# Layer 0's opening products: loads of x in pairs, one modulation run per k tile, and a told order for splits and loads

## The chip, the cores and the metric

The kernel runs on one core of a Trainium2 chip. The metric is device time in microseconds, the median of the runs; a profiled execution of the same program gives the trace. TensorE does the products, VectorE and ScalarE the element-wise work, SyncE issues nearly all loads, and each engine runs its own instructions in order and waits on semaphores for the others.

## What is computed

Two layers of a trunk over 256 latent tokens (x) and 256 context tokens, each 2048 wide. The part that matters here is the front of layer 0: a modulation vector for x and one for the context, the norm, the modulated stream h, and the first columns of h @ w_in.

```python
shift, scale, gate = jnp.split(jax.nn.silu(c) @ w_mod + b_mod, 3, axis=-1)
hx = _rmsnorm(x, norm_w) * (1 + scale[:, None]) + shift[:, None]
a_h, a_b, a_c, a_z, q, k, v, r_z = _split_in(hx @ w_in)
...
mod_c = jax.nn.silu(c_ctx) @ w_mod[:, :n_mod * d] + b_mod[:n_mod * d]
hc = _rmsnorm(ctx, norm_w) * (1 + mod_c[d:2 * d]) + mod_c[:d]
ca_h, ca_b, ca_c, ca_z, cq, ck, cv, cr_z = _split_in(hc @ w_in)
...
y_conv = _conv_branch(a_h, a_b, a_c, a_z, conv_w, conv_norm_w)
x = x + gate[:, None] * (jnp.concatenate([y_conv, y_ret], axis=-1) @ w_out)
```

Conv, retention, w_out and the whole of layer 1 follow, and a last norm.

## The kernel before

**Tiles.** x and the context stand transposed: 16 k tiles (KT) of 128 features by 512 tokens (NT), the first 256 columns x, the others the context. A weight is used as two parts, a high one in fp32r (`whi`, ScalarE's copy of a piece of 1024 columns, 512 at a time) and the rest (`wlo`, VectorE's subtraction); h and y are pairs of the same kind. A product of a 128x128 block of weights with a k tile is three matmuls of 512 columns (`mm3`, L346 to L348): high with high, high with low, low with high.

**The opening (`first_group`, L208).** Seven output tiles of w_in (`p`, in seven PSUM banks) grow side by side over the 16 k tiles, 7 x 16 x 3 = 336 matmuls, while the modulation that h needs is made k tile by k tile. A chunk of the modulation (`MOD_CHUNKS`) has one k tile at both ends and two k tiles between. `mod_step` (L485) multiplies silu(c), silu(c_ctx) with pieces of w_mod as they come, four instructions to a step, each with 32 columns of the array of its own (`tile_position=(0, 32 * j)`) and 256 or 512 columns of weights, in plain fp32; a step reads one piece of 512 KB (`wm`), or two. After four steps ScalarE copies the sums out (`msb`), TensorE transposes them (`modt`, `mod_finish`, L505), and VectorE adds the four parts and the bias (`mv`) and makes the scale (`am`). `h_prep` (L541) then makes xn = x * rstd, scales and shifts it in place per half of the tokens (L548), copies it to h's high part on ScalarE and subtracts for the low part on VectorE (`split`, L368). The statistics (`first_stat`, L458) are 16 squares, summed on VectorE in two sums, and two matmuls with ones.

**Order.** The program names steps; a tile scheduler that puts instructions into an order of its own per engine is free in the whole kernel, so products of p stand between the instructions of one modulation step.

**Loads.** `pump` (L287) issues loads in the order of use (`seq`) into six buffers of 512 KB (`RAW`), each free once its reader is done; splits run up to three pieces ahead (`AHEAD`), with four buffers of high and low halves (`WH`). x comes first, in 16 loads of 256 KB (L387). `load_rest` (L416) fetches constants and a 2 MB broadcast of c and c_ctx (`cb`) at the end of the opening; `silu_rows` (L438) applies silu to it during the first tile behind the opening, since the rows of the later modulation (`mod_row`, VectorE) read it.

**Slots.** x, then yf, x1 and y use 16 slots of 256 KB, one k tile each; h's pairs have 16 of 512 KB.

Of the kernel before, what the change touches and what calls it, by code (L numbers as in the profile page):

```python
# [17 lines left out]
P = 128  # L18
# [65 lines left out]
MOD_CHUNKS = [[0], [1]] + [[2 * i, 2 * i + 1] for i in range(1, 7)] + [[14], [15]]  # L84
# [7 lines left out]
def pack_mod_chunks(w):  # L92
    pieces = []
    for ks in MOD_CHUNKS:
        cols = np.concatenate([mod_tile(w, SCALE + k) for k in ks] + [mod_tile(w, SHIFT + k) for k in ks], axis=1)
        n = cols.shape[1]
        per = 1024 // n
        pieces.append(cols.reshape(KT // per, per, P, n).transpose(0, 2, 1, 3).reshape(KT // per, P, 1024))
    return np.ascontiguousarray(np.concatenate(pieces))
# [24 lines left out]
def layout(x, c, ctx, c_ctx, norm_w, w_mod, b_mod, w_in, conv_w, conv_norm_w, ret_norm_w,  # L124
# [10 lines left out]
    wm = pack_mod_chunks(w_mod[0])  # L135
# [26 lines left out]
    cb = np.concatenate([c[0], c_ctx]).reshape(1, 2 * D)  # L162
# [3 lines left out]
class Trunk:  # L166
    RAW, WH, AHEAD, TMP = 6, 4, 3, 9

    def __init__(self, ctx, tc, io):
# [3 lines left out]
        self.pa = pool("slots", 16)  # L173
# [7 lines left out]
        self.dram = pool("dram", 1, space=bass.MemoryType.DRAM)  # L181

    def slot(self, name, dt=F32):
        return self.pa.tile([P, NT], dt, tag="slot", name=name)
# [12 lines left out]
    def build_program(self):  # L197
# [10 lines left out]
        def first_group():  # L208
            subs = []
            for c, ks in enumerate(MOD_CHUNKS):  # L210
                m = [("M", c, i) for i in range(4)]
                prog.extend(m[:2])
                prog.extend(subs[:-2])
                prog.append(m[2])
                prog.extend(subs[-2:-1])
                prog.extend([m[3], ("MF", c)])
                prog.extend(subs[-1:])
                subs = [("P", 0, k, i) for k in ks for i in range(2)]
            prog.extend(subs)

        for l in range(DEPTH):
            for op in layer_ops(l):
                if op[0] == "P1":
                    if l == 0:
                        first_group()
                    else:
                        prog.extend(("P", 1, k, h) for k in range(KT) for h in range(2))
# [26 lines left out]
        for op in prog:  # L254
            ps = []
            if op[0] == "M":
                n = 2 if len(MOD_CHUNKS[op[1]]) == 2 else 1
                ps = [("wm", (nm + i,)) for i in range(n)]
                nm += n
            elif op[0] == "D":  # L260
                ps = [("wd", (2 * op[1] + op[2],))]
            elif op[0] == "P":
                _, l, k, sub = op
                last = (7 * k + (3 if sub == 0 else 6)) // 8
# [11 lines left out]
        assert nin == [128, 128] and nout == [32, 32] and nm == 64  # L276
# [4 lines left out]
        self.free = [False] * len(seq)  # L281
# [5 lines left out]
    def pump(self):  # L287
        nc = self.nc
        while True:
# [8 lines left out]
            while self.nsplit < 2 * self.nload:  # L298
# [12 lines left out]
                elif s > self.at + self.AHEAD:  # L311
                    break
# [728 lines left out]
```

## Time and profile before

| | |
|---|---|
| median of the runs | 1570.89 us (1570.33 to 1571.09) |
| the profiled execution | 1568.8 us, its span 1567.0 us |
| mean granted TensorE clock | 0.997 |
| TensorE busy | 1535.5 us, 98% of the span |
| VectorE, ScalarE busy | 1153.3 us (74%), 702.0 us (45%) |
| loads and stores | 287.27 MB, mean 183 GB/s |
| loads of x: 16 of 256 KB; of w_mod for the opening: 64 of 512 KB | 5.4 and 6.2 us each to landing |

Times are in us from the first instruction of the span. A busy TensorE is one with a matmul in its pipe: matmuls overlap, and the time that one costs is the distance from its start to the next one's, not its own duration. A plain fp32 instruction leaves two records, so counts of the modulation products are twice the instructions.

### The profile page before, as it was taken

Reading aid. Unit: us, or ns where it says so; the run is one execution under the profiler, and the core shown is the slowest. Engines: PE = TensorE matmul, PEld = TensorE weight load, DVE = VectorE, ACT = ScalarE, POOL = GpSimd, SP = SyncE. Lnnn points to the kernel's source line nnn. Section 1 sums busy time; section 2 is a strip of 40 time slices with the busy share of each in tenths; the row PEclk is TensorE's granted clock in tenths of the full one; section 3 lists DMA queues with packets and bytes.
Section 4 is the critical chain, followed back from the end, with each engine's and each line's share of the span. In section 5 each row is a group of like instructions: output and inputs, shape, how many; then the busy total and the mean of one; then the engine's idle time right before and its main releaser. Section 6 shows DMA issues by size and latency. Waiting matters only on the chain.

```text
span 1567.0 us, 20955 instructions
## 1 busy us (share of the span) xinstructions
PE 1535.5 (98%) x7520; PEld 1252.0 (80%) x7520; DVE 1153.3 (74%) x2241; ACT 702.0 (45%) x1247; POOL 0.7 (0%) x6
## 2 busy tenths in 40 slices
PE   4999999999999999999999999999999999999997
PEld 2546888888888888888888888988888888888886
DVE  4345897777757666676678877889886877677776
ACT  4223432222224454344555332566553565366664
POOL 0000000000000000000000000000000000000000
PEclk9999999999999999999999999999999999999999
DMA  8989566555653233533325776456786434443573
GB/s 328 331 300 331 176 224 191 180 186 189 198 173 124 95 108 96 173 121 95 119 87 183 241 235 217 147 184 212 273 295 202 129 128 133 164 159 110 173 220 106
DMA packets 84633, 287.27 MB, mean 183 GB/s; under 512 B 9392, under 2 KB 13616, under 8 KB 84400
## 3 DMA queue, kind: packets, MB, share of 16 engines
q1 hardware_dynamic: 81648, 282.77, 54.9%
q10 hardware_dynamic: 2880, 3.15, 0.6%
q8 instruction: 59, 0.97, 0.2%
q14 instruction: 46, 0.38, 0.1%
HBM read 281.69 MB, written 4.19 MB: 182 GB/s over the span
## 4 chain that ended last, share of the span: by engine, by line
PE 96%; DVE 1%; DMA 1%; ACT 1%; issue 0%; SPq 0%; DVEq 0%; ACTq 0%
PE acc L346 16%; PE acc L347 16%; PE acc L348 16%; PE acc L353 12%; PE acc L354 6%; PE vps L348 4%; PE vps L346 4%; PE vps L347 4%; PE mod L496 2%; PE p L346 2%; PE p L347 2%; PE p L348 2%; PE p L353 2%; PE ops L353 1%; PE ops L346 1%; PE ops L347 1%
## 5 line engine op out<-in xcount | busy, mean ns | idle before, releaser
L369 ACT ACTIVATE whi<-raw 128x512 fp32r<-128x512 f32 x640 | 401.9, 631 | 657.1 <-PE acc L347 353.3
L370 DVE TENSOR_TENSOR wlo<-raw,whi 128x512 fp32r<-128x512 f32 x640 | 437.2, 688 | 235.2 <-ACT whi L369 220.0
L346 PE MATMUL acc<-h,whi 128*128 128x512 f32 x912 | 355.5, 390 | 0.0
L348 PE MATMUL acc<-h,wlo 128*128 128x512 f32 x912 | 355.2, 390 | 0.0
L347 PE MATMUL acc<-h,whi 128*128 128x512 f32 x912 | 355.2, 390 | 0.0
L353 PE MATMUL acc<-h,whi 128*128 128x512 f32 x656 | 230.2, 394 | 0.0
L348 PEld LDWEIGHTS acc<-h,wlo 128*128 128x128 f32 x912 | 171.2, 188 | 36.0
L346 PEld LDWEIGHTS acc<-h,whi 128*128 128x128 f32 x912 | 171.2, 188 | 34.9
L347 PEld LDWEIGHTS acc<-h,whi 128*128 128x128 f32 x912 | 171.2, 188 | 34.6
L354 PE MATMUL acc<-h,wlo 128*128 128x256 f32 x656 | 184.1, 281 | 0.0
L353 PEld LDWEIGHTS acc<-h,whi 128*128 128x128 f32 x656 | 122.9, 187 | 27.4
L535 DVE CUSTOM_DVE_ANT_0 junk<-raw,cb,sm 128x1024 bf16<-128x1024 f32 x112 | 142.1, 1278 | 0.1
L535 DVE CUSTOM_DVE_ANT_0 junk<-raw,cb,mvp 128x1024 bf16<-128x1024 f32 x112 | 141.8, 1278 | 0.1
L354 PEld LDWEIGHTS acc<-h,wlo 128*128 128x128 f32 x656 | 124.0, 189 | 0.3
L346 PE MATMUL vps<-whi,h 128*128 128x512 f32 x256 | 100.4, 392 | 0.0
L348 PE MATMUL vps<-whi,h 128*128 128x512 f32 x256 | 99.8, 390 | 0.0
L347 PE MATMUL vps<-wlo,h 128*128 128x512 f32 x256 | 99.7, 390 | 0.0
L347 PE MATMUL acc<-y,whi 128*128 128x512 f32 (+1 forms) x208 | 77.7, 374 | 0.0
L348 PE MATMUL acc<-y,wlo 128*128 128x512 f32 (+1 forms) x208 | 77.5, 373 | 0.0
L346 PE MATMUL acc<-y,whi 128*128 128x512 f32 (+1 forms) x208 | 77.5, 373 | 0.0
L353 PE MATMUL acc<-y,whi 128*128 128x512 f32 x176 | 62.2, 399 | 0.0
L348 PEld LDWEIGHTS vps<-whi,h 128*128 128x128 f32 x256 | 48.1, 188 | 10.2
(203 smaller groups left out, 1994.5 us busy)
## 6 DMA issues: line engine op xcount, KB each, us to landing
raw<-wi SPq DMA_DIRECT2D x256, 512.0 KB, 4.0
raw<-wd SPq DMA_DIRECT2D x128, 512.0 KB, 4.2
raw<-wm SPq DMA_DIRECT2D x64, 512.0 KB, 6.2
raw<-wo SPq DMA_DIRECT2D x64, 512.0 KB, 3.9
xs<-xc SPq DMA_DIRECT2D x16, 256.0 KB, 5.4
xr<-xc SPq DMA_DIRECT2D x16, 256.0 KB, 5.4
cb<-cb SPq DMA_DIRECT2D x1, 2048.0 KB, 11.1
scratch<-x ACTq DMA_DIRECT2D x16, 128.0 KB, 3.2
```

The lines of the kernel that those rows point to most:

```text
L346: mm(out, lhsT=whi, rhs=hhi, start=first, stop=False)
L347: mm(out, lhsT=whi, rhs=hlo, start=False, stop=False)
L348: mm(out, lhsT=wlo, rhs=hhi, start=False, stop=last)
L353: mm(out.rearrange("p (s t) -> p s t", s=2), lhsT=w[0], rhs=t[:, :, :NX], start=first, stop=False)
L354: mm(out[:, :NX], lhsT=w[1], rhs=t[:, 0, :NX], start=False, stop=last)
L369: self.nc.scalar.activation(hi, src, AF.Copy)
L370: self.nc.vector.tensor_tensor(lo, src, hi.bitcast(F32), op=ALU.subtract)
L496: nc.tensor.matmul(self.modps[32 * j:32 * j + 32, :n], lhsT=self.csp[:, k, :], rhs=raws[o // 1024][:, o % 1024:o % 1024 + n], start=(i == ...
L535: nc.vector.tensor_tensor_reduce(junk, raw, self.cb[:, D * m + 1024 * hf:D * m + 1024 * hf + 1024], 1.0, init, ALU.mult, ALU.add, out[:, f ...
```

## The change

- x arrives in eight loads of 512 KB; slots are pairs of tiles, eight of 512 KB, given out in halves.
- Every k tile has a modulation chunk of its own: shift and scale side by side, 256 columns, four pieces. Its 16 instructions are held together in program order (`keep_in_program_order`), but for k = 1, whose first piece comes ahead of the first products of p.
- The order of the whole opening is written out (`first_group`) and held on TensorE, VectorE and ScalarE: steps M (modulation run), MF (transposes, sums), H and L (h's high and low part), XN (the norm of one k tile), PP (products of p, a range of the seven tiles), S (which halves of weights may be split by now), W (where a weight piece stands in the order of loads).
- h's high part comes straight from VectorE's scale and shift into the pair; ScalarE makes the same values in fp32 beside it (`p`), and VectorE subtracts for the low part.
- In a step of p the products with h's high part come first, for all its tiles, and those with the low part after them.
- Loads of `wm` may use buffers of others that are not yet in use (`home`): eight pairs until the load order reaches h of k = 8, then four, from k = 12 none, and two more (`vh`, `vl`), one load each.
- The statistics are four sums of four squares with a matmul each; the last square is VectorE's. One matmul on constants (`busy`) follows the first transposes.
- c and c_ctx are loaded once more in a small form at the start, silu is applied to it, and it is stored; the broadcast `cb` reads that, and `silu_rows` is gone.
- Layer 1's products of the same kind are cut 3 + 4 instead of 4 + 3.

```diff
-MOD_CHUNKS = [[0], [1]] + [[2 * i, 2 * i + 1] for i in range(1, 7)] + [[14], [15]]
...
     def slot(self, name, dt=F32):
-        return self.pa.tile([P, NT], dt, tag="slot", name=name)
+        if self.half is None:
+            self.half = self.pa.tile([P, 2, NT], F32, tag="slot", name=name)
+            return self.half[:, 0, :]
+        t, self.half = self.half[:, 1, :], None
+        return t
...
+            M(0), W(0), S(0, 2, True), MF(0), S(0, 6), XN(1), M(1, 0, 1), PP(0, 0, 3), M(1, 1, 4)
+            S(1, 2), PP(0, 3, 5), MF(1), S(1, 6), PP(0, 5, 7)
+            for k in range(1, 5):
+                if k < 3:
+                    W(k)
+                XN(k + 1), PP(k, 0, 3)
+                if k >= 2:
+                    W(k + 1)
+                M(k + 1)
+                if k < 2:
+                    W(k + 1)
+                S(k + 1, 2), PP(k, 3, 5), MF(k + 1), S(k + 1, 6), PP(k, 5, 7)
+            for k in range(5, KT - 1):
+                W(k + 1), M(k + 1), XN(k + 1), PP(k, 0, 3), MF(k + 1), S(k + 1, 6), PP(k, 3, 7)
+            prog.append(("S", None, False))
+            PP(KT - 1, 0, 3), PP(KT - 1, 3, 7)
...
+    def home(self, s):
+        live = [i for i in range(s) if not self.free[i]]
+        here = [self.lent[i] for i in live if i in self.lent]
+        if len(live) - len(here) < self.RAW:
+            return self.praw, "raw"
+        if self.seq[s][0] == "wm":
+            pairs = 8 if s < self.lend[0] else 4 if s < self.lend[1] else 0
+            for pool, tag, n in ((self.pb, "pair", pairs), (self.p1, "vh", 1), (self.p1, "vl", 1)):
+                if here.count(tag) < n:
+                    self.lent[s] = tag
+                    return pool, tag
+        return None, None
...
-        for k in range(KT):
-            t = self.slot("xs")
-            nc.sync.dma_start(t, self.io["xc"][:, k, :])
+        for k in range(0, KT, 2):
+            t = self.pa.tile([P, 2, NT], F32, tag="slot", name="xs")
+            nc.sync.dma_start(t, self.io["xc"][:, k:k + 2, :])
...
+        nc.scalar.dma_start(cs, self.io["cb"])
...
+        nc.scalar.dma_start(self.silu, cs)
+        self.warm_rsqrt(th[:, 0:1])
...
     def first_stat(self):
...
+            if k == KT - 1:
+                nc.vector.tensor_tensor(sq, self.xs[k], self.xs[k], op=ALU.mult)
             else:
-                nc.vector.tensor_tensor(sums[k % 2], sums[k % 2], sq, op=ALU.add)
...
+            if k % 4 == 3:
+                self.keep(ps, lhsT=self.ones, rhs=some, start=(k == 3), stop=(k == KT - 1))
...
     def mod_step(self, idx):
...
+        for i in range(lo, hi):
+            raw = self.piece(s0 + i - lo)
+            for j in range(4):
+                self.keep(self.modps[32 * j:32 * j + 32, :n], lhsT=self.csp[:, 4 * i + j, :],
+                          rhs=raw[:, n * j:n * j + n],
+                          start=(i == 0), stop=(i == 3), tile_position=(0, 32 * j))
+            self.piece_done(s0 + i - lo)
...
+    def busy(self):
+        self.keep(self.bank("acc", "idle")[:, :NX], lhsT=self.ones, rhs=self.csp.rearrange("p k m -> p (k m)")[:, :NX],
+                  start=True, stop=True)
...
+    def h_first(self, k):
...
+        for s, c in enumerate(cols):
+            self.then(nc.vector.tensor_scalar(h[:, 0, c], xn[:, c], am(s), sh(s), op0=ALU.mult, op1=ALU.add))
+        self.hp = self.tmp("p")
+        for s, c in enumerate(cols):
+            self.then(nc.scalar.activation(self.hp[:, c], xn[:, c], AF.Identity, scale=am(s), bias=sh(s)))
+
+    def h_low(self, k):
+        for low in self.held:
+            low()
...
+        self.then(self.nc.vector.tensor_tensor(h[:, 1, :], self.hp, h[:, 0, :].bitcast(F32), op=ALU.subtract))
...
-                if l == 0 and f == A_Z + 1:
-                    for i in range(4 * hf, 4 * hf + 4):
-                        self.silu_rows(i)
```

What it moves, at three places. Names are those of the tiles: st the statistics, mod and modt the modulation's sums and their transposes, p_0 to p_6 the seven output tiles, whi and wlo a weight's parts.

TensorE, from the program's start to the first products of p, before:

```order
L471 MATMUL st<-sq,ones 128x512 x2
L496 MATMUL mod<-raw,csp 32x256 x16
L511 MATMUL modt<-ident,msb 128x128 x2
L496 MATMUL mod<-raw,csp 32x256 x12
L346 MATMUL p_0_286<-h,whi 128x512
L347 MATMUL p_0_286<-h,whi 128x512
```

and now:

```order
L393 MATMUL st<-sq,ones 128x512 x4
L393 MATMUL mod<-raw,csp 32x256 x16
L571 MATMUL modt<-ident,msb 128x128 x2
L393 MATMUL idle<-csp,ones 128x256
L393 MATMUL mod<-raw,csp 32x256 x4
L393 MATMUL p_0_291<-h,whi 128x512
L393 MATMUL p_0_291<-h,wlo 128x512
L393 MATMUL p_1_292<-h,whi 128x512
```

The statistics are four products, one modulation run and one piece of the next stand ahead of p instead of 28 instructions, and the matmul on constants (idle) is new.

TensorE, some k tiles on, in the middle of the opening, before:

```order
L496 MATMUL mod<-raw,csp 32x512 x4
L346 MATMUL p_0_286<-h,whi 128x512
L346 MATMUL p_1_290<-h,whi 128x512
L347 MATMUL p_0_286<-h,whi 128x512
L496 MATMUL mod<-raw,csp 32x512 x2
L348 MATMUL p_0_286<-h,wlo 128x512
L347 MATMUL p_1_290<-h,whi 128x512
L348 MATMUL p_1_290<-h,wlo 128x512
L496 MATMUL mod<-raw,csp 32x512 x2
L346 MATMUL p_2_294<-h,whi 128x512
```

and now (k = 6):

```order
L393 MATMUL mod<-raw,csp 32x256 x16
L393 MATMUL p_0_291<-h,whi 128x512
L393 MATMUL p_0_291<-h,wlo 128x512
L393 MATMUL p_1_292<-h,whi 128x512
L393 MATMUL p_1_292<-h,wlo 128x512
L393 MATMUL p_2_293<-h,whi 128x512
L393 MATMUL p_2_293<-h,wlo 128x512
L393 MATMUL p_0_291<-h,whi 128x512
L393 MATMUL p_1_292<-h,whi 128x512
L393 MATMUL p_2_293<-h,whi 128x512
L571 MATMUL modt<-ident,msb 128x128 x2
L393 MATMUL p_3_327<-h,whi 128x512
```

Before, four instructions of a step stand two and two with products of p between; now the 16 of a k tile stand together, and the transposes come after the first nine products.

VectorE, from the first norm of a k tile to the second, before:

```order
L545 TENSOR_TENSOR xn<-xs,rstd 128x512
L515 TENSOR_REDUCE mv_140<-modt 128x2 x2
L517 TENSOR_TENSOR mv_140<-mv_140,sm 128x2 x2
L522 SCALAR_TENSOR_TENSOR am_143<-mv_140,sm 128x2
L548 TENSOR_SCALAR xn<-xn,am_143,mv_140 128x256 x2
L370 TENSOR_TENSOR h<-xn,h 128x512
L370 TENSOR_TENSOR wlo<-raw,whi 128x512 x2
L545 TENSOR_TENSOR xn<-xs,rstd 128x512
```

and now:

```order
L533 TENSOR_TENSOR xn<-xs,rstd 128x512
L574 TENSOR_REDUCE mv_134<-modt 128x2x2
L577 TENSOR_TENSOR mv_134<-mv_134,sm 128x2x2
L589 SCALAR_TENSOR_TENSOR am_137<-mv_134,sm 128x2
L631 TENSOR_SCALAR h<-xn,am_137,mv_134 128x256 x2
L330 TENSOR_TENSOR wlo<-raw,whi 128x512
L641 TENSOR_TENSOR h<-p,h 128x512
L330 TENSOR_TENSOR wlo<-raw,whi 128x512
L533 TENSOR_TENSOR xn<-xs,rstd 128x512
```

The scale and shift now write h itself, the sums of shift and scale are one instruction each, and the first weight's low part has moved in front of h's low part.

## Rows read from the trace of the kernel before

**Rows 1.** Waits of TensorE, 160 to 1567: who for whom, total, times, longest.

```profile
PE st L480 <- DVE ssq L865: 2.0, 2, 1.6
```

**Rows 2.** Stretches: us, busy us (instructions) of each engine, granted clock, DMA share, GB/s.

```profile
10.00:20.00 10.00, 3.27 (x4) 1.17 (x4) 7.32 (x11) 7.64 (x12) 0.00 (x0) 1.00 1.04 404
...
20.45:27.60 7.15, 4.22 (x59) 1.76 (x58) 3.98 (x12) 3.01 (x6) 0.00 (x0) 1.00 0.97 372
...
27.60:156.10 128.50, 126.94 (x636) 72.34 (x637) 56.36 (x139) 32.43 (x56) 0.00 (x0) 0.99 0.89 318
...
27.83:31.25 3.42, 3.42 (x9) 2.67 (x9) 1.65 (x3) 0.25 (x1) 0.00 (x0) 0.50 1.01 400
...
156.10:1567.00 1410.90, 1400.66 (x6824) 1176.73 (x6822) 1082.03 (x2065) 653.11 (x1164) 0.00 (x0) 1.00 0.52 168
```

**Rows 3.** Tile p: duration ns min/median/max, first and last start, forms.

```profile
L346 PE MATMUL p<-h,whi x112: 389/396/632, 27.6 to 155.4; 128*128 128x512 f32 x112
...
L348 PE MATMUL p<-h,wlo x112: 387/393/632, 29.3 to 155.9; 128*128 128x512 f32 x112
```

**Rows 4.** Timeline, first product of the next tile: start, us, instruction.

```profile
150.18 0.40 PE L346 MATMUL acc<-h,whi 128*128 128x512 f32 x1
```

**Rows 5.** Groups by line and form, 20 to 151: busy us, mean ns | idle before.

```profile
L496 PE MATMUL mod<-raw,csp 128*32 128x512 f32 x192 | 33.2, 603 | 0.1
...
L496 PE MATMUL mod<-raw,csp 128*32 128x256 f32 x128 | 9.0, 395 | 1.0 <-DMA raw<-wm 1.0
```

**Rows 6.** Timeline of TensorE: half a step, then three pieces, then one.

```profile
49.63 1.05 PE L496 MATMUL mod<-raw,csp 128*32 128x512 f32 x4
...
50.61 0.50 PE L348 MATMUL p<-h,wlo 128*128 128x512 f32 x1
...
142.81 1.50 PE L496 MATMUL mod<-raw,csp 128*32 128x256 f32 x24
...
144.24 0.50 PE L346 MATMUL p<-h,whi 128*128 128x512 f32 x1
...
147.19 0.64 PE L496 MATMUL mod<-raw,csp 128*32 128x256 f32 x8
...
147.76 0.50 PE L346 MATMUL p<-h,whi 128*128 128x512 f32 x1
```

**Rows 7.** Timeline of the start: squares, statistics, modulation, norm, first h.

```profile
8.53 8.11 ACT L463 ACTIVATE sq<-xs 128x512 f32<-128x512 f32 x12 [0.20 <-DMA xs<-xc]
...
16.73 3.78 PE L471 MATMUL st<-sq,ones 128*128 128x512 f32 x4 [16.73 <-DVE sq L467]
...
20.45 2.18 PE L496 MATMUL mod<-raw,csp 128*32 128x256 f32 x32
...
20.55 0.69 ACT L433 ACTIVATE rr<-st,eps 128x512 f32<-128x512 f32 x1 [2.40 <-PE st L471]
...
23.39 0.69 DVE L545 TENSOR_TENSOR xn<-xs,rstd 128x512 f32<-128x512 f32 x1
...
24.00 0.23 DVE L515 TENSOR_REDUCE mv<-modt 128x2 f32<-128x8 f32 x2
...
24.58 0.73 DVE L548 TENSOR_SCALAR xn<-xn,am,mv 128x256 f32<-128x256 f32 x2
```

**Rows 8.** Timeline of one chain from msb to the scaled tile, k = 14.

```profile
140.44 0.38 ACT L503 ACTIVATE msb<-mod 128x256 f32<-128x256 f32 x1 [4.63 <-PE mod L496]
...
141.10 0.38 PE L511 MATMUL modt<-ident,msb 128*128 128x128 f32 x2
...
141.24 0.48 PE L346 MATMUL p<-h,whi 128*128 128x512 f32 x1
...
142.12 0.74 DVE L548 TENSOR_SCALAR xn<-xn,am,mv 128x256 f32<-128x256 f32 x2
```

**Rows 9.** Waits in the opening: SyncE for buffers, ScalarE for weight pieces.

```profile
SPq L294 <- PE mod L496: 87.0, 40, 4.4
...
ACT whi L369 <- DMA raw<-wi: 23.3, 10, 5.6
```

More of the change, by code (lines that the diff above doesn't have):

```diff
@@ L89, in mod_tile, with pack_mod_pairs @@
     return w[:, P * f:P * f + P]
-def pack_mod_chunks(w):
+def pack_mod_pairs(w):
     pieces = []
[L94 to L98, printed above, removed]
+    for k in range(KT):
+        cols = np.concatenate([mod_tile(w, SHIFT + k), mod_tile(w, SCALE + k)], axis=1)
+        pieces.append(cols.reshape(KT // 4, 4, P, 2 * P).transpose(0, 2, 1, 3).reshape(KT // 4, P, 1024))
     return np.ascontiguousarray(np.concatenate(pieces))
@@ L226, in build_program @@
                     else:
[L227 removed]
+                        prog.extend(("P", 1, k, lo, hi) for k in range(KT) for lo, hi in ((0, 3), (3, 7)))
                     prog.append(("PE", l))
@@ L281, in build_program @@
         self.free = [False] * len(seq)
+        self.lent = {}
+        self.allow, self.hold, self.held = -1, False, []
+        self.lend = [self.first[prog.index(("H", k))] for k in (8, 12)]
         self.at = self.wused = self.wsplit = 0
@@ L290, in pump @@
             did = False
-            while self.nload < len(self.seq) and (self.nload < self.RAW or self.free[self.nload - self.RAW]):
+            while self.nload < len(self.seq):
+                pool, tag = self.home(self.nload)
+                if pool is None:
+                    break
                 kind, i = self.seq[self.nload]
-                t = self.praw.tile([P, 1024], F32, tag="raw", name="raw")
+                t = pool.tile([P, 1024], F32, tag=tag, name="raw")
                 nc.sync.dma_start(t, self.io[kind][i])
@@ L304, in pump @@
                     lo = self.pw.tile([P, 512], F32R, tag="wlo", name="wlo")
-                    self.split(self.raw[s][:, 512 * hf:512 * hf + 512], hi, lo)
+                    src = self.raw[s][:, 512 * hf:512 * hf + 512]
+                    self.then(nc.scalar.activation(hi, src, AF.Copy))
+                    low = lambda: self.then(nc.vector.tensor_tensor(lo, src, hi.bitcast(F32), op=ALU.subtract))
+                    if self.hold:
+                        self.held.append(low)
+                    else:
+                        low()
                     self.parts[s, hf] = (hi, lo)
@@ L339, in block_done, with then, keep, mm3 @@
             self.pump()
-    def mm3(self, out, w, h, first, last):
+    def then(self, ins):
+        if self.allow is not None:
+            self.tc.keep_in_program_order(ins)
+    def keep(self, *args, **kwargs):
+        self.tc.keep_in_program_order(self.nc.tensor.matmul(*args, **kwargs))
+    def mm3(self, out, w, h, first, last, mm=None):
         (whi, wlo), (hhi, hlo) = w, h
-        mm = self.nc.tensor.matmul
+        mm = mm or self.nc.tensor.matmul
         mm(out, lhsT=whi, rhs=hhi, start=first, stop=False)
@@ L567, in p1_step @@
     def p1_step(self, op):
-        _, l, k, sub = op
-        n = NT if l == 0 else NX
-        for i in range(4) if sub == 0 else range(4, 7):
+        _, l, k, lo, hi = op
+        blocks, h = [], self.h[k]
+        for i in range(lo, hi):
             if k == 0:
```

191 lines of the change are left out of this document (109 added, 82 removed).

## The prediction

> **What bounds the kernel now.** I read first who makes TensorE wait once layer 0's opening products are over. From 160 us to the end its longest wait is for the sum of squares of the last norm, 2.0 us in two waits [rows 1]. From 156.10 us on it is busy 1400.66 of 1410.90 us at a granted clock of 1.00 [rows 2], and from there the programs of before and after stand in the same order on every engine. What the change is worth is therefore the time at which the opening products end. The tile p has its first and last starts at 27.6 and 155.9 us [rows 3]; with 0.25 us for the last product the opening ends at 156.1. From 150.18 us [rows 4] the scheduler has put five products of the next tile in between; at 0.246 us each (below) they are 1.2 us that a later stage is spared, so the opening ends in effect at **154.9 us**.
>
> Inside it TensorE is called busy 126.94 of 128.50 us [rows 2], so the loss is not in waits but in what it is busy with. The modulation products take 33.2 us (512 columns) and 9.0 us (256 columns) [rows 5]. Each instruction leaves two records, so a step of four leaves eight; groups counted x4 are half a step. Such a half has TensorE from 49.63 to 50.61, 0.98 us for two instructions, while a lone 256-column piece, four instructions, takes 147.19 to 147.76, 0.57 us, and three in a row 142.81 to 144.24, 1.43: each further piece adds 0.43, and the four of a k tile take 1.86 us [rows 6]. The code gives each of the four instructions of a group its own 32 columns of the array; they run side by side, and a group cut in two by products of p pays its time twice.
>
> **The change part by part.**
>
> 1. *Start.* The last square of before ends at 8.53 + 8.11 = 16.64 us and takes 0.63, so the last x piece is there by 16.0 [rows 7]. In 512 KB loads x is there between 14.5 us (at 404 GB/s [rows 2] all the way) and 16.0 (no gain); I take 15.3. ScalarE's table load moves ahead of the squares, into the wait for the first x. Then one square on ScalarE, 0.63 (the last is VectorE's, beside it), and two additions of 0.69 (as xn, 128x512 [rows 7]): 17.3 us. The statistics become four products instead of two, but three run while x still lands; one remains, half of 3.78 us: 19.2. From the end of these products to the end of xn before has 16.73 + 3.78 = 20.51 to 23.39 + 0.69 = 24.08 [rows 7], 3.57 us: 22.8. The first modulation run (2.18 us [rows 7]) goes beside it, 19.2 to 21.4, its copy and its transposes are done by 22.5. From the reduce to the end of the scaled tile before needs 24.00 to 24.58 + 0.73 = 25.31 [rows 7]; two small instructions fewer save 0.1, and h's high part is now that very tile, without ScalarE's copy: 24.0. The first weight is the fifth piece, landing at 15.3 + 5 x 1.30 = 21.8, where before it came eighth. **First product of p at 24.1 us, not 27.6**; the second waits for the low half of the weights, told behind h on VectorE: 0.69 less one product, 0.45 us.
>
> 2. *A k tile, steady.* Twelve products of p between two modulation runs take 144.24 to 147.19, 2.95 us, 0.246 each with the changes of tile [rows 6]. A k tile: 21 x 0.246 = 5.17, one run 1.86, two transposes 0.14 (141.10 to 141.24 [rows 8]): **7.17 us**. Fifteen of them and the last 21 products: 15 x 7.17 + 5.17 = 112.7; one piece of the run for k = 1 is done before the first p (-0.4): 112.3 us.
>
> 3. *The pinned chain.* TensorE may no longer run something else while it waits. From the transposes to the scaled tile: 141.10 to 142.12 + 0.74 = 142.86, 1.76 us [rows 8]. For k up to 5 its cover is the transposes and six products, 0.14 + 6 x 0.246 = 1.62: 0.1 us exposed, five times, 0.5. From k = 6 twelve products and a run cover it, 4.8 us: nothing. The copy msb, 140.44 and 0.38 long, let the transposes go at 141.10 [rows 8]; it has six products or more as cover: nothing. h's low part is wanted six products (1.5 us) after the high one and costs VectorE 0.69: nothing.
>
> 4. *Supply.* A k tile needs four modulation pieces and 7/8 of a weight piece, 4.875 pieces of 512 KB. At 404 GB/s [rows 2] a piece is 1.30 us and a k tile 6.3 us, under 7.17. SyncE waited 87.0 us for modulation products to free a buffer [rows 9]; the lent buffers make 16 of six until k = 8, then 12, then 8. So the queue can run at its rate, but the lead is thin at first: from k = 6 on the run comes ahead of the p of two k tiles before, at 24.55 + 5 x 7.17 = 60.4, and wants its 35th piece by 61.8; that lands at 15.3 + 35 x 1.30 = 60.8.
>
> 5. *Clock.* TensorE, busy 4.22 of 7.15 us before the first p, then ran at half clock for 3.42 us [rows 2], 1.7 us lost. The idle product and the shorter gap may keep the full clock, or not: 0 to 1.7. For this and the thin lead I charge 1.0 us, about the middle.
>
> 6. *Off the path.* The silu of the broadcast rows goes from VectorE and ScalarE, behind a TensorE that did not wait for them there [rows 1]: nothing. Slots in pairs free later, but what reads them is over long before: nothing.
>
> Sum: 24.1 + 0.45 + 112.3 + 0.5 + 1.0 = 138.4 us against 154.9: **16.5 us less**. The profiled execution took 1568.8 us (span 1567.0), so 1552.3 by it; it lies 2.1 under the median of the runs, 1570.89, from which I forecast **1554.4 us**. Own range: down by 0.8 (x), 1.0 (no charge), 0.5 (chain) and 0.1 us a k tile (1.5), to 1550.6; up by 0.7 (x), 0.7 (clock), 1.5, and some 3 where loads are late, to 1560.3.
>
> **The rivals.**
>
> *A. Loads set the pace.* If deep prefetch lifts the rate only half of the way from the opening's 318 GB/s to 404 [rows 2], to 361, a piece is 1.45 us. The 35th lands at 66.1, 4.3 us late; the 78th at 128.4, after which 42 products (10.3) and 0.4 remain, 139.1, so the early lateness counts: 1558.7. At the old 318 GB/s (1.65 us) the 78th lands at 144.0, the end is 154.7, and nothing is gained: 1570.7. For it: 318 is what the stage got. Against: SyncE's waits for buffers [rows 9], and 404 when it had them.
> That the row shows 404 GB/s over ten microseconds speaks against the half-way case. The Trainium skill, "DMA: Bandwidth & Descriptors", section "Bandwidth", speaks for it: HBM, not the fabric, binds such loads, at about 358 GB/s for one core. By that rule a piece would take 1.46 us and the end be that of the half-way case within half a microsecond; the trace contradicts the rule over this stretch.
>
> *B. Slower: pinned splits wait for weight loads in front of the chain.* On ScalarE and VectorE a weight split now has a told place ahead of the next reduce. Before, ScalarE waited 23.3 us for weight pieces, ten times [rows 9], while TensorE ran other products. If all of that now holds back the chain, and so TensorE, 23.3 less 16.5 is 6.8 us slower: 1577.7. It decides once a weight piece comes later than its split's place by more than the cover, over 1.1 us on each of 15 k tiles. Against: from k = 3 on its load is issued ahead of the modulation pieces of its step.
>
> *C. The gain is lost behind the opening*, since VectorE cannot run the next stage as early: 1571. Against: VectorE is busy 1082.03 of 1410.90 us there [rows 2] and TensorE hardly waits [rows 1].
>
> **How the numbers follow.** Forecast 0.78; A half-way 0.12; A at the old rate 0.04; C 0.02; B 0.04. A measurement of this kernel tells about 0.2%, 3.1 us, from no change. Faster: 0.78 + 0.12 = 0.90; same: 0.04 + 0.02 = 0.06; slower 0.04. The range, 1550 to 1561, holds the forecast's own and A's half-way case; 0.10 of other cases and the forecast's tails lie outside.
>
> **What would show it.** Right: first p near 24 us, last near 138; modulation near 30 us of TensorE in 16 runs; no 3.4 us of half clock behind the first p; TensorE's order and density unchanged behind the opening. Wrong: modulation runs waiting for raw pieces at k from 2 to 6 (A); p waiting for h, or msb and the reduce standing behind a split, k after k (B); new waits of TensorE after 140 us (C).

## The result and the profile after

The changed kernel takes **1552.09 us** (median of five runs, 1551.13 to 1555.74) against 1570.89: ratio 0.988, 95% interval 0.9869 to 0.9891. The profiled execution took 1552.0 us, span 1550.2 us. The rows below are those of after that answer to [rows 2 to 9].

Stretches of the changed kernel (us, busy us of TensorE, its weight loads, VectorE, ScalarE, GpSimd, granted clock, DMA share, GB/s): the loads of the start, the time up to the first p, the products of p, and all that follows, as in [rows 2].

```profile
10.00:20.00 10.00, 8.38 (x21) 2.10 (x22) 5.68 (x9) 5.34 (x10) 0.00 (x0) 1.00 1.03 412
...
24.07:137.62 113.55, 112.70 (x838) 77.96 (x839) 59.20 (x143) 40.48 (x79) 0.00 (x0) 1.00 0.94 361
137.62:1550.20 1412.58, 1402.58 (x6829) 1177.86 (x6827) 1076.12 (x2048) 648.06 (x1156) 0.00 (x0) 1.00 0.52 168
```

The opening ends at 137.62 us where it ended in effect at 154.9: 17.3 us. What follows takes 1412.6 us, before 1410.9 and the 1.2 us of five products done early, 1412.1: the whole gain lies in the opening and stays. There is no stretch at half clock behind the first p (before, 3.42 us).

Tile p and the groups of the opening (columns as in [rows 3] and [rows 5]):

```profile
L393 PE MATMUL p<-h,whi x224: 387/392/501, 24.1 to 137.4; 128*128 128x512 f32 x112
```

```profile
L393 PE MATMUL mod<-raw,csp 128*32 128x256 f32 x512 | 32.2, 391 | 0.6 <-DMA raw<-wm 0.6
```

The modulation costs 32.2 us of busy TensorE instead of 33.2 + 9.0.

The start, from the last statistics product to the second p (start, us, instruction, idle time before and what ended it), as in [rows 7]:

```profile
15.25 1.41 DVE L524 TENSOR_TENSOR sq<-sq 128x512 f32<-128x512 f32 x2
...
16.71 2.08 PE L393 MATMUL st<-sq,ones 128*128 128x512 f32 x2 [0.81 <-DVE sq L524]
...
18.72 2.82 PE L393 MATMUL mod<-raw,csp 128*32 128x256 f32 x32
...
21.66 0.69 DVE L533 TENSOR_TENSOR xn<-xs,rstd 128x512 f32<-128x512 f32 x1
...
22.14 0.41 PE L571 MATMUL modt<-ident,msb 128*128 128x128 f32 x2 [0.60 <-ACT msb L563]
...
23.19 0.73 DVE L631 TENSOR_SCALAR h<-xn,am,mv 128x256 fp32r<-128x256 f32 x2
...
24.07 0.47 PE L393 MATMUL p<-h,whi 128*128 128x512 f32 x1 [0.52 <-DVE h L631]
...
24.58 0.50 PE L393 MATMUL p<-h,wlo 128*128 128x512 f32 x1
```

TensorE in one k tile that is still short of cover (k = 3), in one with full cover, and at the only run behind the first p that waits for a piece (k = 14):

```profile
41.05 1.93 PE L393 MATMUL mod<-raw,csp 128*32 128x256 f32 x32
42.91 0.50 PE L393 MATMUL p<-h,whi 128*128 128x512 f32 x1
...
45.56 1.16 PE L393 MATMUL p<-h,whi 128*128 128x512 f32 x3
46.56 0.39 PE L393 MATMUL p<-h,wlo 128*128 128x512 f32 x1
...
48.49 1.72 PE L393 MATMUL mod<-raw,csp 128*32 128x256 f32 x28
...
77.14 0.50 PE L393 MATMUL p<-h,whi 128*128 128x512 f32 x1
...
84.24 0.50 PE L393 MATMUL p<-h,whi 128*128 128x512 f32 x1
...
117.94 1.50 PE L393 MATMUL mod<-raw,csp 128*32 128x256 f32 x24
120.00 0.64 PE L393 MATMUL mod<-raw,csp 128*32 128x256 f32 x8 [0.57 <-DMA raw<-wm]
120.57 0.50 PE L393 MATMUL p<-h,whi 128*128 128x512 f32 x1
```

A run takes 41.05 to 42.91, 1.86 us. The k tile from 77.14 to 84.24 takes 7.10 us; the one from 41.05 to 48.49 takes 7.44, because three products that start at 45.56 need 1.00 us up to the next one instead of 0.7: the first product of the new h waits there, 0.3 us. The run at 117.94 takes 2.63 us, as its last piece is 0.8 us late.

SyncE's waits for a modulation product to free a buffer, 18 to 150 us, answer to [rows 9]:

```profile
SPq L315 <- PE mod L393: 27.8, 15, 6.0
```

The loads in two stretches of equal length, one while they still run one behind the other and one when they wait for buffers (columns as above, the last is GB/s):

```profile
60.00:80.00 20.00, 20.00 (x161) 13.82 (x160) 10.05 (x26) 6.52 (x13) 0.00 (x0) 1.00 1.03 412
...
100.00:120.00 20.00, 19.44 (x152) 13.38 (x150) 10.59 (x26) 6.67 (x13) 0.00 (x0) 1.00 0.76 271
```

### The profile page after: what moved, and what is told of

Its sections match the earlier page's. It is cut to its first block, busy times and chain, and to the rows that moved or that the text cites. A ratio compares the mean times of both kernels' runs of the same rounds, so it can differ in the third digit from the quotient of the medians.

```text
span 1550.2 us, 21351 instructions
## 1 busy us (share of the span) xinstructions
PE 1527.7 (99%) x7718; PEld 1259.7 (81%) x7718; DVE 1149.2 (74%) x2224; ACT 703.7 (45%) x1261; POOL 0.7 (0%) x6
## 4 chain that ended last, share of the span: by engine, by line
PE 96%; DVE 1%; DMA 1%; ACT 1%; SPq 0%; issue 0%; DVEq 0%; ACTq 0%
PE acc L399 16%; PE acc L398 16%; PE acc L400 16%; PE acc L405 12%; PE acc L406 6%; PE p L393 5%; PE vps L400 4%; PE vps L399 4%; PE vps L398 4%; PE mod L393 2%; PE p L405 2%; PE ops L405 1%; PE ops L398 1%; PE ops L399 1%; PE p L406 1%; PE ops L400 1%
## 5 line engine op out<-in xcount | busy, mean ns | idle before, releaser
L393 PE MATMUL p<-h,whi 128*128 128x512 f32 x224 | 78.2, 406 | 0.8 <-DVE h L631 0.5
```

The lines of the kernel that those rows point to most:

```text
L393: self.tc.keep_in_program_order(self.nc.tensor.matmul(*args, **kwargs))
```

## The experiments

The experiments ran on three occasions and the changed kernel on one of its own, each time beside the kernel before, so ratios are compared. "x" is the landing of the last x piece, "first p" and "end of p" are the bounds of the opening's products, all in us from the profiled execution; the rate is that of the loads between the two. Where products of the next tile were done early, their time is taken off in brackets. The kernels b are edits of the kernel before, those with e of the changed one.

| kernel | ratio, 95% interval | x | first p | end of p | GB/s |
|---|---|---|---|---|---|
| before | 1 | 15.9 | 27.6 | 156.1 (154.9) | 318 |
| changed | 0.988 [0.9869, 0.9891] | 14.1 | 24.1 | 137.6 | 361 |
| b1_ktiles | 0.9997 [0.9987, 1.0007] | 16.1 | 28.5 | 156.6 (154.6) | 321 |
| b2_lend | 0.9956 [0.9941, 0.9972] | 16.6 | 29.8 | 151.7 (150.5) | 336 |
| b3_lendk | 1.0011 [1.0001, 1.0021] | 15.9 | 34.3 | 158.0 (157.0) | 315 |
| e1_halves | 0.9984 [0.9975, 0.9994] | 14.4 | 25.0 | 152.3 | 322 |
| e2_nolend | 1.0026 [1.0011, 1.0040] | 15.2 | 25.4 | 157.4 | 310 |
| e3_free | 0.9954 [0.9936, 0.9972] | 14.8 | 30.4 | 146.8 | 337 |
| e4_copyh | 0.9934 [0.9920, 0.9949] | 15.4 | 26.8 | 145.1 | |
| e5_x256 | 0.9912 [0.9896, 0.9927] | 15.8 | 25.8 | 139.3 | |
| e6_noidle | 0.9912 [0.9894, 0.9930] | 15.2 | 24.9 | 139.9 | |
| e7_silu | 0.9912 [0.9895, 0.9930] | 15.6 | 25.6 | 139.6 | |
| e8_more | 0.9862 [0.9845, 0.9880] | 15.2 | 24.0 | 135.9 | |
| e9_two | 0.9921 [0.9904, 0.9937] | 14.2 | 25.1 | 143.0 | 346 |

The theory at the outset was the prediction's: TensorE's cut modulation groups were the loss, whole groups are the gain, and buffers need only not get in the way. The main rival was that the loads carry it.

**b1_ktiles: the modulation's form alone, in the kernel before.**

```diff
-MOD_CHUNKS = [[0], [1]] + [[2 * i, 2 * i + 1] for i in range(1, 7)] + [[14], [15]]
+MOD_CHUNKS = [[k] for k in range(KT)]
```

> The kernel before with a single edit: every chunk of the modulation has one k tile, 256 columns. Loads, splits, statistics, h and the free scheduler stay. In its order no group of four is cut any more; the modulation stands in 24 single groups, 9 runs of two, 6 of three and one of four. Theory (cut groups are what the modulation lost): by 0.57, 1.00, 1.43 and 1.86 us a run the modulation takes 24 x 0.57 + 9 + 6 x 1.43 + 1.86 = 33 us instead of 42, so some 8 us of the 17 come from this edit alone: about 1563 us, with the first product of p still near 27.6 us. Rival (the gain is the told order, not the form of the modulation): no more than 2 us, 1569 to 1571.

1570.07 us: nothing gained. The stretch of p in this kernel:

```profile
28.50:156.56 128.06, 124.13 (x830) 75.48 (x831) 59.56 (x169) 32.64 (x62) 0.00 (x0) 0.99 0.90 321
```

TensorE is busy 124.13 us instead of 126.94, and the stretch is 128.06 long instead of 128.50. The modulation products of this kernel:

```profile
L496 PE MATMUL mod<-raw,csp 128*32 128x256 f32 x512 | 36.8, 393 | 0.2 <-DMA raw<-wm 0.2
```

From start to start, the modulation costs 5.7 us less in the stretch, not 8. The products of p, between which the modulation still stands in 38 places (before, in 34), cost 1.8 more, the waits are 2.1 longer, and the transposes and products of the next tile take 1.3 more. So the theory's price was too high, and what was won is lost again beside it. The loads ran at the old rate (321 GB/s, before 318), but that they set the end isn't shown: TensorE waited 0.2 us for modulation pieces in all.

**e2_nolend: the changed kernel with six buffers.**

```diff
-            pairs = 8 if s < self.lend[0] else 4 if s < self.lend[1] else 0
-            for pool, tag, n in ((self.pb, "pair", pairs), (self.p1, "vh", 1), (self.p1, "vl", 1)):
+            for pool, tag, n in ():
```

> The changed kernel without lent buffers: raw pieces have their six buffers as before, the told order stays. Theory (TensorE sets the pace; a buffer freed at one run lands its next piece within the 7.1 us to the next run): only the start suffers, where fewer pieces are there when the first runs want them, 1 to 5 us, 1553 to 1557. Rival (deep prefetch carries the gain): each run waits for its last pieces, 1 us or more per k tile, so the opening loses 15 us or more: 1567 and up.

1573.51 us: the whole gain is gone, so the rival's number came. TensorE's waits from 18 to 158 us, and one run in the middle:

```profile
PE mod L392 <- DMA raw<-wm: 13.5, 16, 3.4
```

```profile
65.72 0.64 PE L392 MATMUL mod<-raw,csp 128*32 128x256 f32 x8 [0.22 <-DMA raw<-wm]
66.91 0.64 PE L392 MATMUL mod<-raw,csp 128*32 128x256 f32 x8 [0.55 <-DMA raw<-wm]
68.18 0.64 PE L392 MATMUL mod<-raw,csp 128*32 128x256 f32 x8 [0.63 <-DMA raw<-wm]
69.54 0.90 PE L392 MATMUL mod<-raw,csp 128*32 128x256 f32 x8 [0.72 <-DMA raw<-wm]
```

The four pieces of one run start 1.2 to 1.4 us apart, at the pace of the loads, and not 0.43. The opening ends 19.8 us later than the changed kernel's: beside these waits, the first p is 1.3 us later, and the granted clock is 0.50 from 69.78 to 73.19, behind such waits, which costs 1.7.

**e9_two: eight buffers (vh and vl lent, no pairs).**

> The changed kernel with two lent buffers (vh, vl), none of the pairs: eight buffers instead of 16, 12 and 8. With six the period of a k tile was (157.35 - 24.1 - 5.4) / 15 = 8.5 us: a run's four buffers are reloaded only as it frees them, some 4.2 us to the first landing and 1.28 us for each further piece. Theory (the number of loads in flight sets that period; each further buffer takes one piece time, 1.28 us, off it until 7.1 us is reached): 8.5 - 2.56 = 5.9, under 7.1, so nearly the whole gain is kept: 1552 to 1557. Rival (the deep lead gathered before the first p, some ten pieces more, is what carries the stage): half of the gain or less is left, 1562 or more.

1559.23 us, between the two: neither number came. The period theory is right in kind (six buffers end at 157.4, eight at 143.0, 16 to 8 at 137.6) and too simple in size:

```profile
PE mod L392 <- DMA raw<-wm: 3.5, 6, 1.3
```

None of these waits is before 62 us: they begin with the run of k = 6, the first one that is told ahead of all products of p of the k tile before and not behind nine of them, so that its pieces are wanted earlier.

**b2_lend and b3_lendk: lending in the kernel before**, b3 also with one k tile to a chunk (both edits above).

> The kernel before, with the lending of free buffers (16, then 12, then 8 buffers of 512 KB instead of six) and nothing else: two k tiles to a chunk, cut groups, free order stay. Theory (two things together carry the gain: cheap modulation runs, and loads that are there for them): TensorE was busy 126.94 of 128.50 us in the old opening, so more buffers can give back only its waits, 1.6 us, and the late first p stays: 0 to -2 us, 1569 to 1571. Rival (the loads alone were the bound; the run without lending came out at 1573.5): most of the gain appears here, 1558 or less.

> The kernel before with both: one k tile to a chunk (256 columns) and the lending of free buffers; the order stays free, x in 256 KB loads, h through ScalarE's copy. One k tile to a chunk alone gave 1570.07, because loads then set the pace (7.4 to 8.5 us a k tile). Theory (the two must come together): 15 k tiles at 7.2 to 7.7 us instead of 8.5, the end of p 8 to 14 us earlier, less the 3.5 us of the late first p: 1558 to 1563. Rival (without the told order the scheduler cuts the groups again or puts splits ahead of the chain): 1567 or more.

b2 gained 6 us, 4 more than the theory and far less than its rival; b3 gained nothing, as the rival had it. In b2 a bare chain, a whole step alone (eight records, four instructions), and a chunk of two k tiles in one piece:

```profile
43.09 0.66 PE L529 MATMUL modt<-ident,msb 128*128 128x128 f32 x4 [0.71 <-ACT msb L521]
...
92.91 1.07 PE L514 MATMUL mod<-raw,csp 128*32 128x512 f32 x8
93.90 0.50 PE L364 MATMUL p<-h,whi 128*128 128x512 f32 x1
...
96.61 3.64 PE L514 MATMUL mod<-raw,csp 128*32 128x512 f32 x32
```

With the pieces at hand the 16 instructions of 512 columns stood together here and took 3.58 us to the next product, 1.79 a k tile. So 512 columns are no dearer than 256. A step alone takes 0.99 us, as much as half a step in [rows 6]: being cut and being alone were dear. Only the number of buffers differs from the kernel before, and the scheduler's order is another: the modulation stands in 18 places between the products of p instead of 34, and the steps of 512 columns keep TensorE busy for 24.3 us instead of 33.2 [rows 5].

```profile
L514 PE MATMUL mod<-raw,csp 128*32 128x512 f32 x192 | 24.3, 598 | 2.0 <-PE modt L529 1.2 <-issue 0.6 <-DMA raw<-wm 0.2
```

So more buffers lightened TensorE, which the theory had left out. This is although the first p came 2.2 us later and the clock stood at 0.50 for 6.8 us, up to 35.96 (before, 3.4). But with pieces at hand the free order also ran modulation ahead with nothing beside the chain. In b3 TensorE from 43 us on, and ScalarE ahead of the first p:

```profile
43.78 0.44 PE L529 MATMUL modt<-ident,msb 128*128 128x128 f32 x2 [0.51 <-ACT msb L521]
44.59 1.93 PE L514 MATMUL mod<-raw,csp 128*32 128x256 f32 x32 [0.38 <-PE modt L529]
```

```profile
32.59 1.15 ACT L387 ACTIVATE whi<-raw 128x512 fp32r<-128x512 f32 x2 [3.57 <-DMA raw<-wi]
33.64 0.61 ACT L387 ACTIVATE h<-xn 128x512 fp32r<-128x512 f32 x1
```

Each of five such chains between 43 and 74 us takes 1.5 us (0.87 from the run's last product to the transposes, 0.65 from the second transpose to the next run), 7.6 in all, of which TensorE is idle for 4.4, and the first p waits until 34.3, since h's copy stands on ScalarE behind the split of a weight piece that lands at 32.6.

**e3_free: the changed kernel, order left to the scheduler** (`then` and `keep` no longer hold anything).

```diff
-        if self.allow is not None:
-            self.tc.keep_in_program_order(ins)
+        return ins
...
-        self.tc.keep_in_program_order(self.nc.tensor.matmul(*args, **kwargs))
+        self.nc.tensor.matmul(*args, **kwargs)
```

> The changed kernel with the order left to the scheduler: nothing is held in program order, all else (x, lending, one run per k tile, h from VectorE) stays. In the built order the whole run of k = 1 then stands ahead of the first p, and the runs of k = 2 and 3 one behind the other ahead of the p of k = 1, each with its transposes at once. Theory (the told order is worth the chains that it covers): 12 instructions more ahead of the first p, 12 x 0.107 = 1.3 us and the wait for their pieces, about 1; two chains without cover of 1.5 us each (0.87 + 0.65, as in the kernel with lending and one k tile to a chunk), and h behind the second, 1.8: 5 to 7 us slower than the changed kernel, ratio 0.991 to 0.993. Rival 1: the order is worth nothing once the pieces are there, within 1 us, 0.988. Rival 2: it carries as much as it seemed to in the kernel with lending and free order (1573.4): 0.998 or more.

1562.48 us, 0.0074 of 1570 or 11.6 us above the changed kernel's ratio; the end of p is 9.1 us later. Between the theory's 5 to 7 and rival 2, and mostly at a place that none of them named: VectorE ahead of the first h, and TensorE behind it with its clock.

```profile
28.27 1.29 DVE L330 TENSOR_TENSOR wlo<-raw,whi 128x512 fp32r<-128x512 f32 x2 [2.19 <-ACT whi L329]
29.48 0.73 DVE L630 TENSOR_SCALAR h<-xn,am,mv 128x256 fp32r<-128x256 f32 x2
...
30.36 0.77 PE L392 MATMUL p<-h,whi 128*128 128x512 f32 x1 [3.37 <-DVE h L630]
```

```profile
30.36:34.43 4.07, 4.07 (x10) 3.20 (x11) 0.58 (x1) 0.00 (x0) 0.00 (x0) 0.50 1.03 412
```

h's scale could go at 23.7, when its factor `am` was there, but four weight splits stand ahead of it, the last two behind ScalarE's copies at 27.6. The first p is 6.3 us late, 0.7 of it by x. TensorE, idle for 3.4 us, then runs at the half granted clock up to 34.43, which costs 2.0 us.

**e1_halves: each run in half groups**, columns 0 and 1 of all four pieces, then 2 and 3.

```diff
-            for j in range(4):
...
+        for js in ((0, 1), (2, 3)):
+            for i in range(lo, hi):
+                for j in js:
```

> The changed kernel with the 16 instructions of a run in another order: first the two left column groups of all four pieces, then the two right ones. Same instructions, same run, no product of p between. Theory (a group of four runs side by side, and half a group costs as much): a run takes eight half groups of 0.43 us, 3.5 us instead of 1.86, on 15 k tiles that stand on the path: 25 us more, about 1577 us. Rival (a run's cost is the change between kinds of products, or the engine overlaps halves by itself): within 2 us of the changed kernel's 1552.

1567.99 us, 16 above the changed kernel's ratio (0.0104 x 1570). A run and the next product:

```profile
43.34 2.82 PE L393 MATMUL mod<-raw,csp 128*32 128x256 f32 x32
46.09 0.50 PE L393 MATMUL p<-h,whi 128*128 128x512 f32 x1
```

2.75 us instead of 1.86, 14.2 us in 16 runs, and the end of p is 14.6 later: the cut costs, at about half of what was expected. The modulation records of this run in its first two thirds (us, busy us and records of TensorE, its weight loads and ScalarE, granted clock, DMA share, GB/s; records that cross an edge count on both sides):

```profile
43.34:44.22 0.88, 0.88 (x8) 0.49 (x10) 0.00 (x0) 1.00 1.03 410
44.22:45.12 0.90, 0.90 (x18) 0.58 (x16) 0.00 (x0) 1.00 1.03 410
```

The left halves follow one another every 0.43 us, as whole groups do in the changed kernel, so half a group does cost as much as a whole one. But from 44.23 on the first two right halves run beside the last two left ones, which the theory had left out: the run takes the time of six halves and not of eight. With products of p on both sides, as in the kernel before, a half has nothing beside it (0.98 us for half a step of 512 columns, [rows 6]).

**e4_copyh: h's high part through ScalarE's copy again.**

```diff
-            self.then(nc.vector.tensor_scalar(h[:, 0, c], xn[:, c], am(s), sh(s), op0=ALU.mult, op1=ALU.add))
+            self.then(nc.vector.tensor_scalar(self.hp[:, c], xn[:, c], am(s), sh(s), op0=ALU.mult, op1=ALU.add))
+        self.then(nc.scalar.activation(h[:, 0, :], self.hp, AF.Copy))
```

> The changed kernel with h's high part made as before: VectorE scales and shifts into a temporary tile, ScalarE copies that to h, VectorE subtracts. Theory (the pinned chain is covered from k = 6 on and exposed before): 0.7 us more at the first product of p and at each of the next five k tiles, 3.5 to 4.5 us in all, 1556; nothing at k = 6 and later, where 12 products and a run stand over it. Rival 1 (the chain is covered everywhere): under 1 us. Rival 2 (the chain counts at every k tile): 0.7 x 16 = 11 us, 1563.

1560.05 us, 8.5 above the changed kernel's ratio; the end of p is 7.5 later. The first product of a new h, k = 3:

```profile
44.12 0.50 PE L393 MATMUL p<-h,whi 128*128 128x512 f32 x1 [0.70 <-ACT h L633]
```

The four k tiles with little cover take 8.1 us instead of 7.4, 2.6 in all, and those behind them 7.12 as before but for the one of k = 14: the place is the theory's, with four k tiles and not five. The first p is 2.7 later, 1.3 of it by x. So 1.4 and 2.6 us are the chain's, 4.0 in all, as expected. The rest is not the chain's: the wait at k = 14 is 0.8 longer, and 1.3 is TensorE's clock behind the first p.

```profile
27.11:30.52 3.41, 3.41 (x9) 2.27 (x7) 1.52 (x3) 0.12 (x1) 0.00 (x0) 0.50 1.02 406
```

The first nine products take 3.8 us instead of 2.6, at the half granted clock, though this kernel has the product on constants. Ahead of them TensorE was busy 1.41 of 3.06 us, from 23.70 on.

**e5_x256, e6_noidle, e7_silu: three small parts undone** (x in 256 KB loads; no product on constants; silu behind the opening).

> The changed kernel with x in 16 loads of 256 KB again, into the halves of the same buffers. Theory (the start is a chain from the last x piece): the last x lands at 15.9 us, as in the kernel before, instead of 14.06, and statistics, h and the first p follow 1.9 us later; the end too, since nothing behind takes it back: ratio 0.9892, 1.9 us over the changed kernel. Rival (the first modulation run and its pieces set the first p): the pieces land 1.9 us later too, but the chain from the run to h is shorter, so under 0.7 us.

> The changed kernel without the product on constants behind the first transposes. Theory (TensorE was busy enough from the first modulation run on): no half clock, 0 us, 0.988. Rival (the idle product keeps the clock through the wait for h): a stretch at 0.50 granted clock behind the first p as in the kernel before, 3.4 us long, 1.7 us more, 0.989.

> The changed kernel with the broadcast rows read from c as it comes and silu applied behind the opening again, eight pieces during the first tile there. Theory (off the path): 0 us, 0.988. Rival (VectorE, 76% busy behind the opening, is late with the first tiles by the 8 x 1.4 us or so of the silu): up to 3 us of TensorE waits between 140 and 200 us, 0.990.

All three came out at 0.9912, just above the changed kernel's interval. Three unlike edits with one number, on an occasion on which the changed kernel itself was not run and x landed 1.1 to 1.7 us later in all three: the times can't tell what of it is the edits. The traces can in part. The end of p is 1.6 to 2.2 us later than the changed kernel's, of which 0.9 to 1.8 is there at the first p already; the rest is the wait at k = 14, whose k tile takes 7.73, 9.17 and 8.37 us (7.87 in the changed kernel). Without the product on constants, from the first p on, the clock is full:

```profile
24.94:30.40 5.46, 5.42 (x39) 3.44 (x40) 2.66 (x5) 1.64 (x4) 0.00 (x0) 1.00 1.03 411
```

So in this execution it wasn't what kept the clock: TensorE was busy 2.26 of the 3.82 us ahead of the first p. One of e6's other three executions has a lower mean clock (0.994 against 0.998); where it lost it isn't known. With silu behind the opening, 140 to 200 us, the row of e6 first and that of e7 below it:

```profile
140.00:200.00 60.00, 60.00 (x267) 49.67 (x266) 46.50 (x80) 21.01 (x37) 0.00 (x0) 1.00 0.55 185
```

```profile
140.00:200.00 60.00, 60.00 (x267) 49.67 (x266) 53.59 (x95) 25.30 (x45) 0.00 (x0) 1.00 0.56 187
```

VectorE does 7.1 us more and TensorE doesn't stop for it. As for x: with 512 KB loads the last piece landed between 14.06 and 15.61 us in the nine kernels that have them (mean 14.9), with 256 KB loads between 15.75 and 16.64 in five (mean 16.1). The larger loads are some 1.2 us earlier, but e5's 15.75 lies so near to e7's 15.61 that its end of p (139.3) isn't later than theirs. This price stays open within 0 to 1.9 us.

**e8_more: three small additions.**

```diff
+                for _ in range((1, 1, 2, 0)[k // 4]):
+                    self.busy()
...
-            pairs = 8 if s < self.lend[0] else 4 if s < self.lend[1] else 0
+            pairs = min(8, KT - self.seq[s][1][0] // 4)
...
-                S(k + 1, 2), PP(k, 3, 5), MF(k + 1), S(k + 1, 6), PP(k, 5, 7)
+                S(k + 1, 2), PP(k, 3, 4), MF(k + 1), S(k + 1, 6), PP(k, 4, 7)
```

> The changed kernel with three small additions: products on constants behind the first three statistics products (TensorE's clock full when the last one and the first modulation run come), lent pairs falling one by one from k = 8 (8, 7, ... instead of 8, 4, 0), and for k up to 4 four tiles of p instead of two behind the transposes. Theory: the fourth statistics product starts at 16.7 and with the run behind it takes 2.0 + 2.8 us, about 1 us of it by the clock; the only wait of a run for its pieces is 0.95 us at k = 15; of the k tiles 1 to 4 each takes 7.43 instead of 7.10 us, 1.3 us in all. If all three come, 3 us less than the changed kernel, ratio 0.986; if the start is set by x and the norm chain alone, 1.5 us. Rival: 0, or slower where the longer stretch of products behind the transposes delays the next run's pieces: 0.988 or more.

1550.65 us, the lowest of all, though its interval overlaps that of the changed kernel. Its start:

```profile
16.16 1.03 PE L393 MATMUL idle<-csp,ones 128*128 128x256 f32 x4
17.87 1.12 PE L393 MATMUL st<-sq,ones 128*128 128x512 f32 x2 [0.69 <-DVE sq L524]
18.93 2.08 PE L393 MATMUL mod<-raw,csp 128*32 128x256 f32 x32
```

The last statistics product takes 1.06 us to the next start instead of 2.01, the run behind it 2.08 instead of 2.82. From x's last landing to the first p (23.96) are 8.8 us instead of 10.0; x landed 1.1 us later in this execution, so the first p is only 0.1 earlier. No run behind the first p waits for its pieces any more (the expectation puts the changed kernel's wait at k = 15; it stood at k = 14), and a k tile short of cover takes 7.1 to 7.3 us instead of 7.4: the end of p is 1.75 us earlier in spite of x.

No run takes apart the order of high and low products within a step, the slots in pairs, or the form of the statistics by itself.

## Where the prediction was right, and where not

- **Total.** 1554.4 us forecast, 1552.09 measured, within the range. By the profiled executions 16.5 us were forecast and 1568.8 - 1552.0 = 16.8 came. The other 2 us are the profile of before, which lay 2.1 under its median while that of after lies on it.
- **Start.** The first p came at 24.07, forecast 24.1, by errors that cancel. x was there at 14.06, not 15.3, the earliest of the nine kernels with such loads (mean 14.9). The sums took 2.6 us from there, not 2.0, as VectorE's last square stood behind an addition. The first run took 2.82 us, not 2.18, since it began at the half clock (before, the clock was full from 21.0 on, most of the run); the transposes and the reduce came 0.3 later for it. With the clock full throughout, e8 needs 8.8 us from x to the first p, which is the forecast's own distance.
- **A k tile.** Forecast 7.17, measured 7.10. The 112.3 us of steady work are the sum's best term.
- **The pinned chain.** The place was right but for one k tile, the size was not: 0.3 us a k tile, not 0.1, in four k tiles (k = 1 to 4) and not five, since the run of k = 6 already covers the chain of k = 5. e4 lengthened the chain and gave 0.7 more in just these k tiles; e8 gave it more cover.
- **Supply.** The rate was right: pieces land 1.28 us apart (forecast 1.30), 409 GB/s, for as long as there are buffers. The run of k = 6 stands ahead of the p of one k tile before, not two, but its forecast start was worked out for the right place, and its thin lead did no harm; the 0.8 us came at k = 14, where no pair is lent any longer. The charge of 1.0 us was met by this wait and not by the clock.
- **What bounds the kernel.** Here the reading failed in part, and the total doesn't show it. "So the loss is not in waits but in what it is busy with" fits the trace of before, and e1 bears out that cut groups are dear. But it took a busy TensorE for the one bound, and used the row on SyncE's 87.0 us of waits [rows 9] only to argue that loads would not be late. e2 kept all the rest of the change and got nothing without the lent buffers; there the loads set the pace. b2 got 6 us from the buffers alone, and in it they lighten TensorE, as the scheduler cuts the groups less. b1 got nothing from the form alone. So the lent buffers are a condition of the gain. Whole groups (e1), buffers (e2) and the told order (e3) each take more than half of the gain away when they are left out, so it can't be shared out among them. That loads and TensorE bounded the old opening at the same length would explain b1, but isn't shown, as TensorE waited 0.2 us for modulation pieces there.
- **The told order.** Priced as a cost alone (a wait that nothing fills). e3 shows that it is worth 8 to 9 us of the opening once pieces lie ready, since the scheduler, left free, puts splits in front of h and runs modulation with its chain bare.
- **Clock.** No half clock behind the first p, as hoped for, but the product on constants isn't the reason: e6 kept the full clock without it, and e4 fell to the half clock with it. What kept it stays open.
- **Silu.** Nothing, as forecast (e7). The sentence that both programs stand in the same order on every engine behind the opening is not exact for this reason: VectorE has 2048 instructions there, before 2065.
- **Rival A** (loads set the pace) is what the kernel does with six buffers (e2) and not with 16. Its half-way case needed 361 GB/s as the queue's limit; 361 is indeed the mean of the stretch, but only because the loads are done early and then wait: while they run they land at 409. The 358 GB/s that the prediction took from the Trainium skill ("DMA: Bandwidth & Descriptors", section "Bandwidth") is by the same section what each core gets when both cores that share the memory stream, so it did not speak for the half-way case; this kernel runs on one core and loaded at 409. The Trainium skill's page "Perfetto Trace Analysis", section "Roofline", says that a core whose neighbour is idle can pull more than that share, up to about 435 GB/s, and the 409 agrees with this.
- **Rival B** (weight splits in front of the chain) did not come with the told order. It came where the order is free, in b3 and e3, at the first h.
- **Rival C.** 1412.6 us behind the opening against 1412.1: nothing lost.

## What to carry to other kernels

When a busy engine is fed by a queue that waits for buffers, the engine's own trace is not enough: work out the stage's time from the loads as well, with the buffers that they have, and test each half of the change alone. Here the lighter engine work alone gave nothing (b1), and the buffers alone a third of the gain (b2). With deep prefetch a free scheduler can run early what has its data early, in front of the chain that everything waits for (b3, e3), so lend buffers and tell the order in one step. Groups of instructions that share the array side by side should stay together: cutting them was dear at 256 columns (e1) and at 512 [rows 6].

## What was not expected of the hardware

- The trace's first record of the granted clock, to full, stands at 20.57 us in the changed kernel and at 15.46 in e8, which has products on constants between the statistics. Ahead of it the stretch rows print 1.00, but a plain fp32 product of 512 columns takes 2.01 us there, and 1.06 in e8: the row can't be trusted ahead of the first record. In e9 the first record stands at 12.63, and the stretch in which the same product takes 2.01 us and the first run 3.64 is printed as the half clock:

```profile
16.05:22.87 6.82, 5.65 (x34) 1.89 (x34) 2.82 (x5) 1.59 (x3) 0.00 (x0) 0.50 1.03 411
```

- Eight same loads of x end between 14.06 and 15.61 us from execution to execution; the first lands at 4.9 to 5.2 in all, the second at 6.4 to 7.9. A start can't be forecast closer than that.
- Half a step of 512 columns costs 0.98 us with products of p on both sides, as much as a whole step alone (0.99). In e1, at 256 columns, half groups of the same columns follow one another every 0.43 us, as whole groups do, but two halves of different columns run side by side.
